# A larger part of a second stream's mixer is moved from ahead of a conditional to beside the experts behind it

## The chip, the core and the metric

One Trainium2 chip, one NeuronCore of it. The program is one launch: all weights and inputs lie in HBM, and the result goes back there. The metric is the device time of one execution in microseconds; a kernel's time is the median of its runs. The profiled execution is one more run, with the hardware profiler on; times inside the program are given in microseconds from its first instruction.

## The reference, cut to what matters

The program is two transformer blocks in a row, all in float32. The first block has two layers; each is an attention and a mixture of 16 experts (a token goes to 2 of them):

```python
for layer in range(DEPTH):
    sh1, sc1, g1, sh2, sc2, g2 = jnp.split(c_act @ w_mod[layer] + b_mod[layer], 6, axis=-1)
    ...
    x = x + g1[:, None, :] * mix
    h = modulate(rmsnorm(x, ffn_norm_g[layer]), sh2, sc2)
    x = x + g2[:, None, :] * grouped_moe(h, router_w, router_bias, exp_w_gate[layer], exp_w_up[layer], exp_w_down[layer])
```

The second block has two streams, `x` (256 tokens, from the first block) and a context `ctx` (256 tokens, an input). Its first layer works on the context by itself:

```python
hc = _rms(ctx, norm_mix_w[l]) * (1.0 + scc1) + shc1
qa_c, ka_c, va_c, qb_c, kb_c, vb_c = heads(hc @ w_in, False)
oa_c = _dense_attend(qa_c, ka_c, va_c, sink)
ob_c = _dense_attend(qb_c, kb_c, vb_c, None)
out_c = jnp.concatenate([oa_c, ob_c], axis=-1) @ w_out
ctx = ctx + gc1 * ac
ctx = ctx + gc2 * _swiglu(_rms(ctx, norm_ffn_w[l]) * (1.0 + scc2) + shc2, ffn_w_in[l], ffn_w_out[l])
```

None of this needs `x`. So the context's mixer (norm, projections, attention, output) and its feed-forward part can run at any time ahead of the second block's attention over both streams.

## The kernel before

The kernel writes its work as Python generators. A generator issues the instructions of a piece and yields a number, the piece's weight. `mix` (L236) takes several generators with a total weight each and always advances the one that is least far along; `upto` (L264) takes from one generator until a weight is used up; `then` runs one after the other; `drain` runs to the end. A scheduler then sets the order on each engine from the order in which instructions were written, their dependences and the buffers that are free. The order is fixed at build time: an engine takes its instructions in that order and waits where an operand is not there.

All weights come through SP's DMA queue, in units of 128 x 1024 float32 (512 KB), into a pool `raw` of eight buffers; a unit can be issued when the work that read the buffer before it is done. `wsplit` (L346) splits a unit into two parts H and L, one instruction on ACT (L356) and one on DVE (L357), and a matrix product `lin` (L371) is three matmuls for each 128 rows (L379 to L381): the high parts, and the two mixed ones. `lin_t` (L399 to L401) is the same with the operands exchanged, used for the values. Modulation vectors are made by `mods` (L553): a group has 16 units, each read by four matmuls straight from `raw` (L562), then one copy (L567) and four transpositions (L570).

The place of the change is the first block's first mixture of experts, in `run` (L1490 to L1501):

- `moe_route` norms `x`, routes each token and loads four units of the first expert pair into buffers of their own, `eraw`.
- `before` gathers the tokens of the first four experts (L907), writes the routing's remainder, drains what it is given as `fill`, loads eight more units of the first pair into `raw`, and calls `overflow` (L991).
- `overflow` is a conditional on all engines: its body runs when an expert got more than 64 tokens. Nothing is moved across it: what is written ahead of it stands ahead of it on every engine. In these inputs its body is jumped over. Its first instructions are the loads of the count `novi` (L1005) and the branch (L1006).
- `experts` runs eight pairs of experts: four bursts of sixteen records for gate and up (L388, out of `eraw` or `raw` into `psE`), an activation, transpositions (L947), two bursts for down, and the scatter back into `x` (L964, L965).

The context's mixer is the generator `con` = `context()`, which runs `even_mixer` (L1232) for `ctx` and then the norm for its feed-forward part. Its pieces, in order, are: the norm and the two projections of the keys (weight 5.3); the values (two units `wevv`, L399 to L401) and the keys' head norms (L1218, L1228; 7.0); the first query, two projections with `wev` units (2.6 each) and their head sums (1.3); then four rounds of attention (scores L1285 into the bank `psS`, transpositions L642, products L620) with the next query beside each, and the output projection with `wevo` units. `cffn.run(1)` is the first part of the context's feed-forward. `chain` holds two groups of modulation vectors, 32 units, whose results are needed later.

In this stage PSUM has three banks `psE`, one `psS` that the modulation groups use too, one `psZ`, and `psN` and `psL` from outside.

Of the kernel before, what the change touches and what calls it, by code (L numbers as in the profile page):

```python
# [235 lines left out]
def mix(*streams):  # L236

    live = [[g, 0.0, float(n)] for g, n in streams if g is not None]
    while live:
        s = min(live, key=lambda v: v[1] / v[2])  # L240
        try:
            n = next(s[0])
            s[1] += n
            yield n
        except StopIteration:
            live.remove(s)


def drain(g):
    for _ in g:  # L250
        pass


def then(*gs):
    for g in gs:
        yield from g
# [7 lines left out]
def upto(n, g):  # L264

    while n > 0:
        v = next(g, None)
        if v is None:
            return
        n -= v  # L270
        yield v
# [16 lines left out]
class Net:  # L288
# [1134 lines left out]
    def run(self, stop=None):  # L1423
# [32 lines left out]
        def hidden(u):  # L1456
            yield from self.swiglu(0, fx[0], fx[1], ctx, mc[0][:, 40:48], u, u + 1)

        cffn = Chain(*((u, hidden(u)) for u in range(11)))
        with ExitStack() as es1:  # L1460
# [11 lines left out]
            with ExitStack() as es:  # L1472
                self.banks(es, M=1, S=2, T=1, V=1)
                self.pools(es, ("big", 1), ("st", 1), ("wk", 1))
                chain = Chain(("gate", mod0([1])), ("c0", mod20([0])), ("m0", mod0([2])), ("c1", mod20([1])),
                              ("kv", self.mods(a["modkv"], [0], self.crep, self.v["bkv"], mk)))
# [7 lines left out]
            def context():  # L1484
                s = dict(x=ctx, m=mc[0], gate=iter(()), fill=iter(()))
                yield from self.even_mixer(self.fp, self.st, s, (kc, vvc), None)
                fx.extend(self.t(self.fp, [P, KD, S], tag, F32R) for tag in ("hh", "hl"))
                self.norm(ctx, KD, self.v["nfw0"], mc[0][:, 32:40], mc[0][:, 24:32], *fx)
# [3 lines left out]
            with ExitStack() as es:  # L1492
                self.banks(es, E=3, Z=1, S=1, M="S", D="S", T="Z", V="L", Y="L")
                self.extra = 4
                self.pools(es, ("eraw", self.extra), ("mo", 1), ("wk", 1), ("st", 1))
                chain = Chain(("c2", mod20([2])), ("m1", mod1([0])))
                con = context()
                drain(self.moe_route(0, self.v["ffng0"], m0))
                before, experts = self.moe_experts(mix((upto(18.0, con), 18), (chain.run(), 47)))
                drain(before)  # L1500
                drain(mix((experts, 196), (then(con, cffn.run(1)), 76)))  # L1501
            if stop == "moe0":
                return
            with ExitStack() as es:
# [3 lines left out]
                chain = Chain(("m1", mod1([1, 2])))  # L1508
# [3 lines left out]
            with ExitStack() as es:  # L1512
# [4 lines left out]
                before, experts = self.moe_experts(cffn.run(5))  # L1517
# [27 lines left out]
        with ExitStack() as es1:  # L1545
# [15 lines left out]
            with ExitStack() as es:  # L1561
# [3 lines left out]
                chain = Chain(("g", mod21([1])), ("f", mod21([2])))  # L1565
# [32 lines left out]
```

## Time and profile before

| | us |
|---|---|
| median of 3 runs | 2150.39 |
| lowest and highest run | 2146.48, 2150.41 |
| the profiled execution | 2157.56 |
| its span, first to last instruction | 2155.8 |
| first expert burst behind the conditional | 326.66 |
| the last expert pair's scatter begins | 677.18 |

In the timeline a row is an engine's stretch of like instructions: start, length, engine, line, operation, what it writes and reads, the count, and in brackets the idle time ahead of it with what ended it. A matmul's length there includes its way through the array; the price of one among many is the distance of their starts. A float32 matmul makes two records. PE is TensorE, PEld its weight loads, DVE VectorE, ACT ScalarE, POOL GpSimd; SPq is a row of SP's queue, an issued transfer.

### The profile page before, as it was taken

What the parts mean: (1) busy time and instruction counts of PE and PEld (TensorE: products, weight loads), DVE (VectorE), ACT (ScalarE), POOL (GpSimd) and SP (SyncE); (2) the same over time, 40 slices, a digit from 0 to 9 for tenths busy, and PEclk for the clock granted to TensorE, in tenths of its full rate; (3) what the DMA queues carried; (4) which work ended last, traced back from release to release, by engine and by line L of the source; (5) the groups of instructions that cost most, each with busy time, mean ns of one, the idle gap of its engine ahead of it and who ended that gap; (6) DMA issues with size and microseconds to landing.
All of it is one profiled execution on the core that took longest, in us unless ns stands there. A gap on an engine that the chain in (4) does not pass through costs nothing.

```text
span 2155.8 us, 35965 instructions
## 1 busy us (share of the span) xinstructions
PE 2006.3 (93%) x13942; PEld 1486.7 (69%) x13942; DVE 1201.8 (56%) x3193; ACT 835.2 (39%) x1580; POOL 134.2 (6%) x152
## 2 busy tenths in 40 slices
PE   5999889999998999999999989997999999998999
PEld 2666664544446877874555358777999777768999
DVE  3644643434345676752433257767777556576776
ACT  2343323433223355531222134755444334444443
POOL 1000200000002110100000014002000100001000
PEclk8999889999999999999999999998999999998999
DMA  9788678768787666438988976103555533224552
GB/s 369 264 301 313 256 255 323 282 248 346 283 349 286 215 224 218 163 130 333 366 345 353 410 277 242 69 20 137 181 185 173 171 139 118 98 94 145 187 183 93
DMA packets 135845, 492.84 MB, mean 229 GB/s; under 512 B 15136, under 2 KB 15536, under 8 KB 135408
## 3 DMA queue, kind: packets, MB, share of 16 engines
q1 hardware_dynamic: 134640, 487.63, 61.7%
q8 instruction: 113, 1.85, 0.3%
q10 hardware_dynamic: 864, 2.53, 0.3%
q0 software_dynamic: 160, 0.27, 0.1%
q14 instruction: 68, 0.56, 0.1%
HBM read 489.32 MB, written 1.05 MB: 227 GB/s over the span
## 4 chain that ended last, share of the span: by engine, by line
PE 48%; DVE 4%; DMA 2%; ACT 1%; issue 1%; POOL 0%; POOLq 0%; ACTq 0%; DVEq 0%
PE psL L379 8%; PE psL L380 8%; PE psL L381 8%; PE psE L388 7%; PE psM L562 1%; PE psS L1390 1%; PE psT L642 1%; PE psS L1285 1%; PE psD L379 1%; PE psD L381 1%; PE psD L380 1%; PE psV L620 1%; DVE L L357 1%; PE psL L399 1%; PE psL L401 1%
## 5 line engine op out<-in xcount | busy, mean ns | idle before, releaser
L379 PE MATMUL psL<-hh,H 128*128 128x256 f32 (+1 forms) x1800 | 535.4, 299 | 12.3 <-ACT H L356 3.4
L357 DVE TENSOR_TENSOR L<-raw,H 128x1024 fp32r<-128x1024 f32 (+1 forms) x336 | 409.7, 1222 | 231.3 <-ACT H L356 221.9
L381 PE MATMUL psL<-hh,L 128*128 128x256 f32 (+1 forms) x1800 | 525.4, 293 | 6.7 <-DVE L L357 6.7
L380 PE MATMUL psL<-hl,H 128*128 128x256 f32 (+1 forms) x1800 | 525.5, 293 | 4.4 <-DVE hl L489 4.0
L356 ACT CAST H<-raw 128x1024 fp32r<-128x1024 f32 (+1 forms) x336 | 347.5, 1039 | 424.3 <-PE psL L380 118.2
L379 PEld LDWEIGHTS psL<-hh,H 128*128 128x128 f32 x1800 | 352.1, 196 | 52.3 <-issue 23.2
L381 PEld LDWEIGHTS psL<-hh,L 128*128 128x128 f32 x1800 | 351.4, 196 | 19.6 <-DVE L L357 10.8
L380 PEld LDWEIGHTS psL<-hl,H 128*128 128x128 f32 x1800 | 351.6, 196 | 14.4 <-issue 5.4
L442 POOL TENSOR_TENSOR sa<-sa,sq 128x256 f32<-128x256 f32 x83 | 72.8, 877 | 1188.4 <-ACT sq L440 776.0
L562 PE MATMUL psM<-raw,crep 128*32 128x256 f32 x1408 | 125.7, 407 | 17.1 <-DVE crep L612 13.3
L388 PE MATMUL psE<-eraw,xg 128*64 128x512 f32 x512 | 125.5, 637 | 3.9 <-PEq L1006 3.8
L388 PE MATMUL psE<-raw,xg 128*64 128x512 f32 x512 | 116.0, 597 | 2.0 <-DMA raw<-in_eu_dram 2.0
L595 ACT ACTIVATE pr<-psS,nm,hr 128x512 f32<-128x512 f32 (+1 forms) x96 | 67.8, 706 | 72.5 <-DVE nm L589 45.2
L379 PE MATMUL psL<-ah,H 128*128 128x256 f32 x296 | 87.0, 297 | 5.8 <-DVE x L1174 2.1
L388 PE MATMUL psE<-raw,at 128*64 128x512 f32 x384 | 89.0, 601 | 2.1 <-ACT at L948 2.1
L388 PEld LDWEIGHTS psE<-eraw,xg 128*64 128x64 f32 x512 | 37.1, 145 | 72.7 <-issue 67.9
L380 PE MATMUL psL<-al,H 128*128 128x256 f32 x296 | 84.4, 286 | 0.7 <-DVE al L369 0.6
L381 PE MATMUL psL<-ah,L 128*128 128x256 f32 x296 | 83.1, 282 | 0.3 <-DVE L L357 0.3
L388 PEld LDWEIGHTS psE<-raw,xg 128*64 128x64 f32 x512 | 34.8, 137 | 65.6 <-issue 59.7
L562 PEld LDWEIGHTS psM<-raw,crep 128*32 128x32 f32 x1408 | 38.7, 113 | 56.5 <-issue 16.4
L586 DVE TENSOR_REDUCE mx<-psS 128x1 f32<-128x512 f32 (+1 forms) x80 | 46.1, 580 | 38.5 <-PE psS L1285 30.0
L379 PEld LDWEIGHTS psL<-ah,H 128*128 128x128 f32 x296 | 56.2, 191 | 13.9 <-DVE ctx L1174 4.7
(404 smaller groups left out, 3470.3 us busy)
## 6 DMA issues: line engine op xcount, KB each, us to landing
raw<-in_mod_dram SPq DMA_DIRECT2D x192, 512.0 KB, 4.8
raw<-in_ed_dram SPq DMA_DIRECT2D x96, 512.0 KB, 9.6
raw<-in_fg_dram SPq DMA_DIRECT2D x66, 512.0 KB, 4.3
raw<-in_fu_dram SPq DMA_DIRECT2D x66, 512.0 KB, 4.1
raw<-in_fo_dram SPq DMA_DIRECT2D x66, 512.0 KB, 3.9
eraw<-in_eg_dram SPq DMA_DIRECT2D x64, 512.0 KB, 7.7
raw<-in_eg_dram SPq DMA_DIRECT2D x64, 512.0 KB, 8.7
raw<-in_eu_dram SPq DMA_DIRECT2D x64, 512.0 KB, 7.4
```

Of the source, the lines that this page charges most:

```text
L356: nc.scalar.copy(h[:, :n], r[:, :n])
L357: nc.vector.tensor_tensor(l[:, :n], r[:, :n], h[:, :n].bitcast(F32), op=ALU.subtract)
L379: mm(ps[:, ns], wh, xh[:, k, ns], start=k == 0, stop=False)
L380: mm(ps[:, ns], wh, xl[:, k, ns], start=False, stop=False)
L381: mm(ps[:, ns], wl, xh[:, k, ns], start=False, stop=k == kt - 1)
L388: self.nc.tensor.matmul(o, w, r, start=start, stop=stop)
L399: mm(ps[:, :n], xh[:, kk, ts], w[0][:, k], start=kk == 0, stop=False)
L401: mm(ps[:, :n], xl[:, kk, ts], w[0][:, k], start=False, stop=kk == last)
L442: (nc.vector if i else nc.gpsimd).tensor_tensor(acc[i], acc[i], sq, op=ALU.add)
L562: nc.tensor.matmul(ps[32 * j:32 * j + 32, 256 * hf:256 * hf + 256], crep[:, k, :], r[:, 256 * j:256 * j + 256], start=k == 0, stop=k == KD ...
L586: V.reduce_max(mx, ps[:, :n], axis=AX.X)
L595: nc.scalar.activation(p, ps[:, :n], AF.Exp, bias=nm, scale=scale, accum_out=sm)
```

## The change

```diff
                 con = context()
                 drain(self.moe_route(0, self.v["ffng0"], m0))
-                before, experts = self.moe_experts(mix((upto(18.0, con), 18), (chain.run(), 47)))
+                before, experts = self.moe_experts(mix((upto(5.0, con), 5), (chain.run(), 47)))
                 drain(before)
-                drain(mix((experts, 196), (then(con, cffn.run(1)), 76)))
+                drain(mix((experts, 196), (then(con, cffn.run(1)), 89)))
```

Before, the pieces of `con` up to the first query's head sums are written ahead of the conditional (5.3 + 7.0 + 2.6 + 2.6 + 1.3 = 18.8). After, only the first piece is (5.3), and the others are written beside the experts. No instruction is added or taken away.

What it does to the order. On PE, ahead of the conditional, the last rows of before are two modulation units, a head sum of the first query, the last unit, its transposition and a score matmul of the context's attention:

```order
L381 MATMUL psL_3294<-hh_2815,L_3291 128x256
L562 MATMUL psS_3180<-raw_3328,crep_108 32x256 x4
L562 MATMUL psS_3180<-raw_3334,crep_108 32x256 x4
L1218 MATMUL psN_3372<-cst_64,sil_3320 128x2 x2
L562 MATMUL psS_3180<-raw_3340,crep_108 32x256 x4
L570 MATMUL psZ_3348<-cst_64,msb_3346 128x128 x4
L1285 MATMUL psS_5994<-kc,ah_3223 128x256
L1005 TENSOR_LOAD novi_2733
L1006 COMPARE_AND_BRANCH
```

Of these rows the query's projection (L381), its head sum (L1218) and the score matmul (L1285) moved behind the conditional.

Now the keys' head norms (sums L1218, spreads L1228) stand among the modulation units, and the last of these come in one row:

```order
L1228 MATMUL psN_5860<-cst_64,hr_5847 64x128 x4
L562 MATMUL psS_3070<-raw_3107,crep_108 32x256 x4
L1218 MATMUL psN_5866<-cst_64,sil_2962 128x2 x2
L562 MATMUL psS_3070<-raw_3113,crep_108 32x256 x4
L1228 MATMUL psN_5883<-cst_64,hr_5870 64x128 x4
L562 MATMUL psS_3070<-raw_3119,crep_108 32x256 x4
L562 MATMUL psS_3070<-raw_3125,crep_108 32x256 x4
L562 MATMUL psS_3070<-raw_3131,crep_108 32x256 x4
L562 MATMUL psS_3070<-raw_3137,crep_108 32x256 x4
L570 MATMUL psZ_3169<-cst_64,msb_3167 128x128 x4
L1005 TENSOR_LOAD novi_2733
L1006 COMPARE_AND_BRANCH
```

Four more such units stand between the last L562 shown and L570. What moved is the work that stood between the units: only the keys' norms are left.

On PE, just behind the conditional, the first burst reads `eraw` in both kernels. Before, a score matmul, a transposition of the context's attention and then the burst of the four `raw` units that were loaded first follow:

```order
L388 MATMUL psE_5985<-eraw_2568,xg_2738 64x512
L388 MATMUL psE_5985<-eraw_2566,xg_2738 64x512
L1285 MATMUL psS_5995<-kc,ah_3223 128x256
L642 MATMUL psZ_6058<-cst_64,pr_6003 128x128
L388 MATMUL psE_5985<-raw_3396,xg_2738 64x512
L388 MATMUL psE_5985<-raw_3394,xg_2738 64x512
```

The context's attention rows between the bursts moved to the second pair and later.

Now the burst of the units loaded last (3183 to 3189) follows at once, then that of the units loaded first (3175 to 3181), then the values:

```order
L388 MATMUL psE_5770<-eraw_2566,xg_2738 64x512
L388 MATMUL psE_5897<-raw_3189,xg_2738 64x512
L388 MATMUL psE_5897<-raw_3187,xg_2738 64x512
L388 MATMUL psE_5897<-raw_3185,xg_2738 64x512
L388 MATMUL psE_5897<-raw_3183,xg_2738 64x512
L388 MATMUL psE_5770<-raw_3181,xg_2738 64x512
L388 MATMUL psE_5770<-raw_3179,xg_2738 64x512
L388 MATMUL psE_5770<-raw_3177,xg_2738 64x512
L388 MATMUL psE_5770<-raw_3175,xg_2738 64x512
L399 MATMUL psL_5791<-H_5781,hh_2815 128x256
L400 MATMUL psL_5791<-L_5782,hh_2815 128x256
L401 MATMUL psL_5791<-H_5781,hl_2816 128x256
```

The values moved here from ahead of the conditional, and the two `raw` bursts changed places.

In SP's queue the value units stood ahead of the last six units of the first modulation group. Now the modulation units and the eight expert units stand there without a break up to SP's load of the count, and behind the conditional come, in this order:

```order
L343 DMA eraw_5906<-in_eu_dram 128x1024
L343 DMA eraw_5908<-in_eu_dram 128x1024
L343 DMA eraw_5910<-in_eu_dram 128x1024
L335 DMA raw_5779<-in_wevv_dram 128x1024
L335 DMA raw_5785<-in_wevv_dram 128x1024
L343 DMA eraw_5912<-in_eu_dram 128x1024
L335 DMA raw_5940<-in_ed_dram 128x1024
```

The value units moved from ahead of the conditional to behind three transfers of the first pair. From the last expert pair's first scatter matmul (677.18 us before) to the end of the program PE's rows are the same in both kernels, and in the same order.

## Rows read from the trace of the kernel before

**Rows 1.** The page: TensorE's row; the two instructions of a weight unit's split.

```profile
PE 2006.3 (93%) x13942; PEld 1486.7 (69%) x13942; DVE 1201.8 (56%) x3193; ACT 835.2 (39%) x1580; POOL 134.2 (6%) x152
L357 DVE TENSOR_TENSOR L<-raw,H 128x1024 fp32r<-128x1024 f32 (+1 forms) x336 | 409.7, 1222 | 231.3 <-ACT H L356 221.9
L356 ACT CAST H<-raw 128x1024 fp32r<-128x1024 f32 (+1 forms) x336 | 347.5, 1039 | 424.3 <-PE psL L380 118.2
```

**Rows 2.** Windows: length; busy PE, PEld, DVE, ACT, POOL; clock; DMA share; GB/s.

```profile
264.00:282.30 18.30, 15.21 (x119) 9.65 (x111) 9.38 (x40) 3.58 (x8) 0.00 (x0) 0.87 0.74 253
282.30:290.93 8.63, 8.63 (x66) 7.33 (x66) 5.66 (x15) 4.70 (x11) 0.00 (x0) 0.88 0.59 194
290.93:304.21 13.28, 12.48 (x134) 9.51 (x131) 4.83 (x21) 2.38 (x5) 0.00 (x0) 1.00 0.69 234
304.21:320.70 16.49, 13.75 (x112) 10.42 (x109) 5.04 (x24) 1.79 (x3) 0.00 (x0) 0.83 0.91 353
320.70:326.66 5.96, 4.54 (x35) 2.22 (x35) 2.49 (x14) 2.03 (x3) 0.00 (x0) 0.79 0.51 190
326.66:677.18 350.52, 328.71 (x1698) 168.68 (x1699) 141.33 (x422) 119.01 (x253) 5.12 (x7) 0.98 0.79 308
```

**Rows 3.** PE's timeline around the conditional: start, length, instruction, count, idle ahead.

```profile
289.91 1.07 PE L562 MATMUL psS<-raw,crep 128*32 128x256 f32 x16
290.93 0.39 PE L399 MATMUL psL<-H,hh 128*128 128x256 f32 x1
...
296.79 0.51 PE L1218 MATMUL psN<-cst,sil 128*128 128x2 f32 x4
...
298.66 0.66 PE L570 MATMUL psZ<-cst,msb 128*128 128x128 f32 x4 [0.80 <-DVE msb L567]
...
300.66 0.66 PE L1228 MATMUL psN<-cst,hr 128*64 128x128 f32 x8
...
324.70 0.66 PE L570 MATMUL psZ<-cst,msb 128*128 128x128 f32 x4 [1.27 <-DVE msb L567]
325.29 1.22 PE L1285 MATMUL psS<-kc,ah 64*128 64x256 f32 x2
326.66 6.34 PE L388 MATMUL psE<-eraw,xg 128*64 128x512 f32 x16
...
337.41 0.70 PE L1285 MATMUL psS<-kc,ah 64*128 64x256 f32 x2
```

**Rows 4.** PE's timeline, a 24-matmul projection and a burst in the experts' stretch.

```profile
605.75 0.39 PE L379 MATMUL psL<-hh,H 128*128 128x256 f32 x1
...
608.82 3.65 PE L388 MATMUL psE<-raw,xg 128*64 128x512 f32 x16
```

**Rows 5.** Transfers: landing time of units issued 282 to 290 us; a full window.

```profile
raw<-in_mod_dram SPq DMA_DIRECT2D x3, 512.0 KB, 3.2
305.00:310.00 5.00, 4.47 (x40) 3.54 (x44) 1.29 (x7) 0.22 (x1) 0.00 (x0) 1.00 1.02 399
```

**Rows 6.** PE's waits, 326.66 to 677.18 us: us in total, times, longest.

```profile
PE psS L1285 <- ACT pr L595: 4.0, 3, 1.7
...
PE psZ L964 <- DVE x L966: 1.9, 7, 0.3
PE psN L964 <- DVE x L966: 1.9, 4, 0.5
PE psN L964 <- ACT mh L959: 1.8, 3, 0.8
```

**Rows 7.** PE's timeline, the last expert pair's first scatter matmul.

```profile
677.18 0.28 PE L964 MATMUL psN<-SG,mh 128*128 128x256 f32 x1
```

## The prediction

> **What bounds the kernel now.** I read the page first, then the windows by stage, then TensorE's timeline on either side of the conditional. The page has PE busy 93% of the span [rows 1], so what decides is where PE's remaining idle time and its slow clock lie, not how much work there is. The stretch that the change touches runs from about 264 us (the router is done, the first gather starts) to 677.18 us, where the last expert pair is scattered back [rows 7]. The windows cut it in two at the conditional [rows 2]. Ahead of it, 264.00 to 326.66, PE is busy 54.6 of 62.7 us (the five rows added). Behind it, 326.66 to 677.18, PE is busy 328.7 of 350.5 us, with the granted clock at 0.98 of full speed and the DMA engines at 0.79: the experts are bound by PE, and a microsecond of PE work that is put there costs about a microsecond. The reader should see two more things. Ahead of the conditional the granted clock falls to 0.83 and 0.79 in the last two rows, and the DMA rate swings between 194 and 353 GB/s: neither PE nor DMA runs full there. And the first burst behind the conditional takes 6.34 us [rows 3], where a burst of the same sixteen records takes 3.65 us later [rows 4]: PE is at 1.2 GHz there and not at 2.4.
>
> From the last pair on, the order of PE's instructions is the same in both kernels. So the whole change is the shift of that one point, 677.18 us: how much earlier the conditional comes, less what the experts' stretch grows by.
>
> **How much earlier the conditional comes.** Before, the context's work between its first two projections and the conditional is: the values (48 matmuls, 290.93 to 296.79 us, 5.9 us), the first query's two projections (48 matmuls) and two small head sums (L1218). Also one score matmul, L1285, at 325.29 us, is ahead of the first burst at 326.66 us [rows 3]. All of it leaves. What stays ahead of the conditional is the norm, the two projections of the keys with their head norms, and all 32 units of the two modulation groups. The change says what it does: the order shows the values and the query behind the conditional, and the head norms of the keys still ahead of it.
>
> I rebuild the new stretch from rows. The context's two key projections end at 289.9 us, where the next modulation rows start [rows 3]; two modulation units now stand ahead of them, and a unit is eight records, so by 1.07 us for sixteen records [rows 3] that is 1.07 us: they end at about 291.0. Behind them stand sixteen modulation units (128 records, 8.6 us), two head sums and two head spreads (0.5 and 0.6 us each, L1218 and L1228), two transpositions of a modulation row (0.6 each, L570) and the two waits for the copy ahead of those (0.80 and 1.27) [rows 3]. That is 8.6 + 3.4 + 2.1 = 14.1, so PE alone would be done at 305.1 us.
>
> The transfers say a little later. There are eight `raw` buffers and two hold the context's norm until about 288 us, so about eight of these sixteen units can be on the way when PE gets to them, and the other eight wait for a buffer. The ninth is issued when the first has been read, about 292.7 us; one alone takes 3.2 us to land [rows 5], so 296 us; the next seven follow at the rate that the DMA engines reach when they are kept full, 399 GB/s [rows 5], which is 1.31 us for 512 KB: 305.2 us. Reading the last (0.5), the copy (1.27) and the transposition (0.6) make 307.6. I take 307.5 us for the first expert burst, **19.2 us earlier**. The bounds are 305.1 (PE alone) and, with the 253 GB/s of the first window [rows 2], 2.07 us for a unit, 310.5 + 2.4 = 312.9: between 21.6 and 13.8 us earlier.
>
> The Trainium skill, DMA: Bandwidth & Descriptors, section "Where 436 GB/s comes from", says that transfers from HBM are held to about 358 GB/s for a core. By that the eight units take 1.46 us each and the conditional would come 1.2 us later. The row has 399 GB/s over 5 us, so the trace does not agree for a stretch of that length.
>
> **What the experts' stretch pays.** PE work at full clock: values 5.9; the query's two projections, by one of 24 matmuls from 605.75 to 608.82 us [rows 4], 6.1; the two head sums 1.1; the score matmul that stood at 325.29 us, 0.7, as the one at 337.41 us takes [rows 3]. Together **13.8 us**. ACT and DVE get four more splits of a weight unit (1.04 and 1.22 us each [rows 1]) and SP four more transfers; ACT is busy 119 and DVE 141 of 350 us there, and the DMA engines are at 0.79 [rows 2], so these are hidden but for the first pair.
>
> At the first pair they are not. The eight units of experts that stand last ahead of SP's branch follow the modulation units through the same buffers: at 1.31 us each the last lands at 305.2 + 8 x 1.31 = 315.7 us. The first burst, from buffers of its own, ends at 307.5 + 6.3 = 313.8 us, and the second now is the one that reads the units loaded last: 1.9 us of waiting. The third ends at 323.0. Then come the 48 matmuls of the values, whose two weight units SP issues behind three transfers into `eraw` and as `raw` buffers come free in the second burst, near 317.5 us; landed 3.2 later and split on ACT and DVE (1.04 + 1.22 [rows 1]), the first is ready at 323.0, and about half a unit later behind the transfers that are queued: 0.6 us. **2.5 us** together. The lower bound is 0; if the first value unit waits for a buffer of the third burst, it is 5.
>
> The rest of the stretch moves both ways. PE's waits there in the row view are 1.9 + 1.9 + 1.8 us ahead of the scatter's first matmuls L964 and 4.0 us ahead of the score matmuls L1285 [rows 6]. Counted in PE's order over the eight pairs, an L964 follows another scatter matmul at once 29 times before and 15 times now, since there is more projection work to put between: 5.6 x 14/29 = 2.7 us less. But two score matmuls that share the one `psS` bank stand within about 2 us of each other five times before and nine times now: 4.0 x 4/5 = 3.2 us more. I set the two at 0.5 us more, with -2.7 and +3.2 as ends.
>
> **The sum.** -19.2 + 13.8 + 2.5 + 0.5 = -2.4 us on the profiled execution, whose span is 2155.8 us and whose time is 2157.56. The median of the runs is 2150.39, 7.2 us less, and the stretch is no different there for all that is known; I put the same shift on it: **2148.0 us**, 0.1% faster. A measurement of this kernel tells about 0.2%, 4.3 us, from no change, so the forecast is "no change".
>
> The Trainium skill, TensorE: Matmul & The Clock Gate, section "Loop structure matters more than you think", says that matmuls which wait for DMA let PE go cold, and that the matmul after it runs cold. That speaks against this change, which makes PE wait for modulation units between 296 and 306 us. Before, the granted clock is 0.79 in the window ahead of the first burst and that burst is slow already [rows 2, 3], so the sum has one slow burst either way; by the rule a second burst at 1.2 GHz would add 6.34 - 3.65 = 2.7 us and make the sum +0.3 us, still no change.
>
> **Rivals.** *The gaps fill (faster).* The conditional comes when PE alone allows it (305.1 us, -21.6), the added projections cover the scatter's waits (-2.7), the score matmuls cost nothing more and the first pair waits 2.5: -21.6 + 13.8 + 2.5 - 2.7 = -8.0 us, 2142.4. For it: the experts' stretch has 21.8 us of idle PE, which is all in small waits, and more independent work stands between them now. Against it: the eight modulation units that must still come through two-thirds of the buffers after 291 us, and the one score bank.
>
> *The transfers set the pace (slower).* From the ninth modulation unit to the value weights, 21 units come through one queue in a row. If they come not at 399 but at the experts' mean of 308 GB/s [rows 2], 1.70 us for a unit, the last modulation unit lands at 307.9 us (+2.7), the last of the eight expert units at 321.5, the second burst starts there, and the five units behind it land at 330, so the values start near 332.3 and not 323.6: +8.7 us, a sum of +6.3 us, 2156.7. It turns slower than 0.2% at about 1.61 us for a unit, 326 GB/s. For it: the mean rates of the rows ahead of the conditional, 253, 194 and 234 GB/s. Against it: in those rows PE held the buffers, and where several transfers were queued the rate was 399.
>
> **How the numbers follow.** Forecast 0.48, filled gaps 0.36, transfers 0.16. The forecast's own range is -7 to +2 us, by the bounds of its terms; a little of it lies past 0.2% on the faster side, and a little of the filled gaps (those under 4.3 us) on this side. So faster 0.40, the same 0.45, slower 0.15. The range reaches from -10 to +5 us, 2140.4 to 2155.4: it leaves out the far end of the filled gaps and most of the slower rival, and takes in the bounds of the unknown terms.
>
> **What would show it.** In the profile of the changed kernel the first burst of L388 behind the conditional should start at 305 to 309 us; the modulation rows ahead of it should show waits on `raw<-in_mod_dram` of a few us in all; a wait on `raw<-in_eu_dram` of 1 to 3 us should stand ahead of the second burst; the values (L399) should run at 323 to 330 us; and the last pair's scatter should start near 675 us. It would be wrong if the first burst started after 311 us (the transfers), if that scatter came before 671 us (the gaps fill), or if the span changed outside this stretch, where the order is the same.

## The result, and the profile after

The changed kernel takes 2169.51 us in the median (2168.22 to 2172.92) where the kernel before takes 2150.1: a ratio of 1.0095, 95% interval 1.0081 to 1.0110. It is 19.4 us, 0.95%, slower; the forecast was 2148.0 and "no change". The profiled execution took 2172.92 us with a span of 2171.1, 15.3 more than the span before; the profiled execution of before is 7 us above its median, that of after 3.4.

First the page: TensorE's row, to be held against [rows 1]. The share is the same, the busy time is 11.5 us more for the same number of instructions.

```profile
PE 2017.8 (93%) x13942; PEld 1490.2 (69%) x13942; DVE 1199.0 (55%) x3193; ACT 834.0 (38%) x1580; POOL 134.9 (6%) x152
```

Then the windows by stage, as in [rows 2] (length; busy PE, PEld, DVE, ACT, POOL; clock; DMA share; GB/s). The cuts are where the context's key projections begin and end, where the last modulation units are waited for, and the first burst behind the conditional.

```profile
264.00:284.30 20.30, 18.04 (x150) 10.85 (x142) 9.99 (x48) 2.88 (x8) 0.00 (x0) 0.84 0.77 253
284.30:295.40 11.10, 11.07 (x56) 8.40 (x56) 5.04 (x14) 3.91 (x10) 0.00 (x0) 0.75 0.46 154
295.40:308.60 13.20, 10.67 (x133) 5.88 (x132) 5.27 (x29) 0.48 (x2) 0.00 (x0) 0.87 0.88 330
308.60:314.40 5.80, 2.57 (x28) 0.90 (x29) 0.87 (x2) 0.00 (x0) 0.00 (x0) 1.00 1.02 412
...
314.42:696.80 382.38, 354.54 (x1804) 186.28 (x1805) 145.78 (x450) 125.25 (x264) 5.78 (x7) 0.94 0.76 290
```

The last row is the experts' stretch, from the first burst to the last pair's first scatter matmul, which stood at 677.18 us before [rows 7]. It is 382.38 us long against 350.52. TensorE is busy 25.8 us more in it and idle 6.0 us more, and the granted clock is 0.94 where it was 0.98 [rows 2].

TensorE's timeline around the conditional, for [rows 3], and at the end of the stretch:

```profile
308.62 0.64 PE L562 MATMUL psS<-raw,crep 128*32 128x256 f32 x8 [0.43 <-DMA raw<-in_mod_dram]
310.31 0.64 PE L562 MATMUL psS<-raw,crep 128*32 128x256 f32 x8 [1.05 <-DMA raw<-in_mod_dram]
311.60 0.64 PE L562 MATMUL psS<-raw,crep 128*32 128x256 f32 x8 [0.65 <-DMA raw<-in_mod_dram]
313.05 0.66 PE L570 MATMUL psZ<-cst,msb 128*128 128x128 f32 x4 [0.81 <-DVE msb L567]
314.42 2.76 PE L388 MATMUL psE<-eraw,xg 128*64 128x512 f32 x11 [0.72 <-PEq L1006]
320.11 2.46 PE L388 MATMUL psE<-eraw,xg 128*64 128x512 f32 x5 [2.92 <-issue]
322.38 7.83 PE L388 MATMUL psE<-raw,xg 128*64 128x512 f32 x32
333.72 0.38 PE L399 MATMUL psL<-H,hh 128*128 128x256 f32 x1 [3.51 <-ACT H L356]
334.98 0.58 PE L400 MATMUL psL<-L,hh 128*128 128x256 f32 x1 [0.87 <-DVE L L357]
...
696.80 0.28 PE L964 MATMUL psN<-SG,mh 128*128 128x256 f32 x1
```

The first burst starts 12.2 us earlier than before. Inside it TensorE stands for 2.92 us with nothing that the profile shows to wait for. The values then wait 3.51 and 0.87 us for the split of their weights. Why the weights are late is on SP's queue:

```profile
306.01 3.09 SPq L335 DMA_DIRECT2D raw<-in_eg_dram  x4
309.19 3.43 SPq L335 DMA_DIRECT2D raw<-in_eu_dram  x4
322.90 2.86 SPq L343 DMA_DIRECT2D eraw<-in_eu_dram  x3
325.87 0.84 SPq L335 DMA_DIRECT2D raw<-in_wevv_dram  x2
```

The value units stand behind three transfers into `eraw`, which go out when the first burst gives its buffers back (322.90 us), and are issued at 325.87, not near 317.5 as forecast. TensorE's waits from the first burst to 696.80 us, for [rows 6]:

```profile
PE psS L1285 <- ACT pr L595: 6.9, 6, 1.8
PE psL L399 <- ACT H L356: 3.5, 1, 3.5
PE psE L388 <- issue: 2.9, 1, 2.9
...
PE psN L964 <- ACT mh L959: 0.3, 1, 0.3
```

The scatter's waits of 5.6 us (L964) are all but gone, and the score matmuls wait 6.9 us for the softmax where they waited 4.0. So far the idle time. The clock is seen when the stretch is cut where it changes. These are windows in which it is low; the long rows between them, 341 to 385, 406 to 450, 454 to 501, 512 to 549 and 556 to 668 us, have 1.00. Two more low windows are not shown: 320 to 324 us, in the first bursts, and 668 to 672 (0.58), behind a wait of 1.29 us for expert weights.

```profile
334.00:341.00 7.00, 6.13 (x29) 6.02 (x29) 2.06 (x2) 2.87 (x4) 0.00 (x0) 0.51 1.03 416
...
385.00:389.00 4.00, 4.00 (x14) 1.73 (x16) 1.93 (x12) 1.70 (x4) 0.00 (x0) 0.57 0.98 393
399.00:406.00 7.00, 5.69 (x15) 2.71 (x17) 1.85 (x8) 2.60 (x8) 0.00 (x0) 0.51 1.00 392
...
450.00:454.00 4.00, 4.00 (x12) 1.08 (x10) 1.39 (x7) 2.50 (x6) 0.00 (x0) 0.57 1.02 419
501.00:512.00 11.00, 10.40 (x24) 3.15 (x26) 3.71 (x12) 3.18 (x11) 0.00 (x0) 0.53 0.79 306
...
549.00:556.00 7.00, 6.52 (x17) 2.47 (x18) 1.43 (x3) 2.43 (x5) 0.00 (x0) 0.51 1.02 411
```

Each of the windows shown follows a wait: the values' at 333.72 us, a wait of 0.68 for the scatter matrix at 384.61, and the score matmuls' of 1.77 (399.63), 0.76 and 1.12 (446.44, 448.92), 1.53 (501.24) and 0.91 us (547.63). One of them in TensorE's timeline:

```profile
497.75 0.70 PE L1285 MATMUL psS<-kc,ah 64*128 64x256 f32 x2
498.37 0.33 PE L947 MATMUL psE<-cst,ga 128*128 128x128 f32 x1
498.63 1.08 PE L620 MATMUL psL<-pt,vvc 128*64 128x256 f32 x6
501.24 1.09 PE L1285 MATMUL psS<-kc,ah 64*128 64x256 f32 x2 [1.53 <-ACT pr L595]
...
508.26 3.61 PE L388 MATMUL psE<-raw,at 128*64 128x512 f32 x8
511.69 3.60 PE L388 MATMUL psE<-eraw,xg 128*64 128x512 f32 x16
```

The second score matmul of a pair follows the first by less than 3 us of other work, finds the one `psS` bank still under the softmax and waits 1.53 us. For the 10 us behind it TensorE runs at 1.2 GHz: eight records of L388 take 3.61 us there, sixteen take 3.60 from 511.69 on.

Not every wait is followed by a low clock. The sixth score wait of the changed kernel, 0.76 us at 594.02, is not: the clock is 1.00 from 556 to 668 us. And of the three in the kernel before only one is:

```profile
436.94 0.70 PE L1285 MATMUL psS<-kc,al 64*128 64x256 f32 x2 [1.70 <-ACT pr L595]
437.57 5.35 PE L388 MATMUL psE<-eraw,xg 128*64 128x512 f32 x16
...
452.34 0.70 PE L1285 MATMUL psS<-kc,ah 64*128 64x256 f32 x2 [1.09 <-ACT pr L595]
452.97 3.65 PE L388 MATMUL psE<-raw,at 128*64 128x512 f32 x16
```

The burst behind the wait of 1.70 us takes 5.35 us, those behind the waits of 1.09 and of 1.20 us (541.59) take 3.65, full speed. What decides this is not shown by any run here.

The account of the +19.6 us at the end of the stretch: the first burst -12.2; moved work at full clock +13.8, as forecast; idle time +6.0; and 25.8 - 13.8 = 12.0 us by which the same matmuls took longer, which is the clock. From that point to the end the rows are the same in both kernels, and yet the changed one takes 4.3 us less there (1474.3 against 1478.6); so the two profiled executions differ by 15.3 us in the end, and that 19.6 comes so near to the 19.4 of the medians is in part chance.

### The profile page after: what moved, and what is told of

Its sections match the earlier page's. It is cut to its first block, busy times and chain, and to the rows that moved or that the text cites. A ratio compares the mean times of both kernels' runs of the same rounds, so it can differ in the third digit from the quotient of the medians.

```text
span 2171.1 us, 35956 instructions
## 1 busy us (share of the span) xinstructions
PE 2017.8 (93%) x13942; PEld 1490.2 (69%) x13942; DVE 1199.0 (55%) x3193; ACT 834.0 (38%) x1580; POOL 134.9 (6%) x152
## 4 chain that ended last, share of the span: by engine, by line
PE 47%; DVE 4%; DMA 1%; ACT 1%; issue 1%; POOL 0%; POOLq 0%; ACTq 0%; DVEq 0%
PE psL L379 8%; PE psL L380 8%; PE psL L381 8%; PE psE L388 7%; PE psM L562 1%; PE psS L1390 1%; PE psT L642 1%; PE psS L1285 1%; PE psD L379 1%; PE psD L381 1%; PE psD L380 1%; PE psV L620 1%; DVE L L357 1%; DMA raw<-in_fg_dram 1%; PE psL L399 1%
## 5 line engine op out<-in xcount | busy, mean ns | idle before, releaser
L381 PE MATMUL psL<-hh,L 128*128 128x256 f32 (+1 forms) x1800 | 524.4, 293 | 5.0 <-DVE L L357 5.0
L381 PEld LDWEIGHTS psL<-hh,L 128*128 128x128 f32 x1800 | 350.2, 195 | 18.1 <-DVE L L357 8.7
L562 PE MATMUL psM<-raw,crep 128*32 128x256 f32 x1408 | 126.5, 411 | 16.3 <-DVE crep L612 13.2
L388 PE MATMUL psE<-eraw,xg 128*64 128x512 f32 x512 | 122.3, 619 | 7.2 <-PEq L1006 4.1
L388 PE MATMUL psE<-raw,xg 128*64 128x512 f32 x512 | 118.4, 607 | 2.4 <-DMA raw<-in_eu_dram 2.4
L388 PE MATMUL psE<-raw,at 128*64 128x512 f32 x384 | 96.6, 640 | 2.2 <-ACT at L948 2.1
L388 PEld LDWEIGHTS psE<-eraw,xg 128*64 128x64 f32 x512 | 36.3, 142 | 73.2 <-issue 68.2
L381 PE MATMUL psL<-ah,L 128*128 128x256 f32 x296 | 83.4, 283 | 0.3 <-DVE L L357 0.3
L388 PEld LDWEIGHTS psE<-raw,xg 128*64 128x64 f32 x512 | 35.9, 139 | 68.7 <-issue 62.0
L562 PEld LDWEIGHTS psM<-raw,crep 128*32 128x32 f32 x1408 | 39.1, 114 | 56.2 <-issue 17.8
L399 PE MATMUL psL<-H,hh 128*128 128x256 f32 x224 | 64.7, 292 | 3.5 <-ACT H L356 3.5
```

Of the source, the lines that this page charges most:

```text
L381: mm(ps[:, ns], wl, xh[:, k, ns], start=False, stop=k == kt - 1)
L388: self.nc.tensor.matmul(o, w, r, start=start, stop=stop)
L399: mm(ps[:, :n], xh[:, kk, ts], w[0][:, k], start=kk == 0, stop=False)
L562: nc.tensor.matmul(ps[32 * j:32 * j + 32, 256 * hf:256 * hf + 256], crep[:, k, :], r[:, 256 * j:256 * j + 256], start=k == 0, stop=k == KD ...
```

## The experiments

Each kernel was timed beside the kernel before. The table has the median, the ratio to before with its interval, and from the profile the start of the first burst behind the conditional, the length from there to the first burst of the second expert layer, TensorE's busy time in it, and the score matmuls' waits for the softmax (rows L1285 or L1283 with ACT pr). The bank edit and the hold are explained below. A profile is one execution; those of "cut 5, weight 100" and "cut 5, bank, values loaded" are of their kernels' shortest execution.

| kernel | us | ratio | first burst | length | busy | score waits |
|---|---|---|---|---|---|---|
| before (cut 18, weight 76) | 2150.1 | | 326.66 | 637.4 | 599.0 | 4.0 |
| changed (cut 5, weight 89) | 2169.5 | 1.0095 [1.0081, 1.0110] | 314.42 | 668.3 | 625.2 | 6.9 |
| changed, once more | 2169.3 | 1.0096 [1.0079, 1.0112] | 313.14 | 665.7 | 624.8 | 6.9 |
| cut 18, weight 89 | 2150.6 | 1.0006 [0.9995, 1.0016] | 324.58 | 636.3 | 600.8 | 1.8 |
| cut 12 | 2149.4 | 0.9999 [0.9987, 1.0011] | 314.20 | 646.6 | 608.6 | 1.8 |
| cut 5, weight 76 | 2177.7 | 1.0124 [1.0105, 1.0143] | 314.08 | 676.2 | 622.1 | 5.0 |
| cut 5, weight 100 | 2164.8 | 1.0075 [1.0058, 1.0092] | 312.16 | 654.4 | 614.2 | 0.6 |
| cut 5, values loaded | 2170.5 | 1.0101 [1.0083, 1.0119] | 314.64 | 665.8 | 624.8 | 6.9 |
| cut 18, bank | 2142.4 | 0.9970 [0.9958, 0.9981] | 325.52 | 626.6 | 593.1 | 1.5 |
| cut 5, bank | 2149.1 | 0.9998 [0.9987, 1.0008] | 314.11 | 646.1 | 612.2 | 0.0 |
| cut 12, bank | 2149.4 | 1.0007 [0.9994, 1.0019] | 313.66 | 640.2 | 602.7 | 0.0 |
| cut 5, bank, values loaded | 2148.9 | 0.9997 [0.9986, 1.0009] | 310.41 | 645.1 | 612.2 | 0.0 |
| cut 5, bank, hold | 2156.4 | 1.0037 [1.0023, 1.0052] | 313.73 | 652.2 | 611.3 | 4.0 |
| **cut 12, bank, hold** | **2134.3** | **0.9936 [0.9920, 0.9953]** | 315.51 | 627.8 | 595.2 | 0.0 |
| cut 18, bank, hold | 2153.2 | 1.0008 [0.9993, 1.0024] | 324.88 | 640.2 | 600.7 | 0.2 |
| cut 12, hold | 2154.0 | 1.0019 [1.0009, 1.0028] | 314.08 | 650.3 | 612.5 | 2.9 |
| cut 5, hold | 2161.2 | 1.0059 [1.0037, 1.0082] | 311.89 | 653.9 | 614.7 | 5.5 |

**Half of the change, and the weight alone.** Two theories stood at the start: F, that the loss is made at the first pair by the values, and C, that it is made all along the stretch by the attention's waits and the clock.

```
cut 12:              upto(12.0, con), 12   ...   then(con, cffn.run(1)), 82
cut 18, weight 89:   upto(18.0, con), 18   ...   then(con, cffn.run(1)), 89
```

> Half of the change: the cut stands at 12 and the weight of the context's stream is 82, so the two value units and their 48 matmuls stay ahead of the conditional and only the first query, its head sums and the first score matmul go beside the experts. Theory F (the loss of the full change is made at the first pair: 2.92 us of idle TensorE in the first burst, 3.51 and 0.87 us ahead of the values, and values at 1.2 GHz): all of that is tied to the values, so this kernel is 2 to 7 us faster than the kernel before. Theory C (the loss is made all along the experts' stretch, where TensorE falls to 1.2 GHz after waits of the context's attention): the attention still begins later and is still packed closer than before, so 3 to 9 us slower than before, and the granted clock of the experts' stretch is near 0.95 rather than 0.98.

> The kernel before with the weight 89 for the context's stream instead of 76 and nothing moved across the conditional: the stream is paced 17% faster against the experts. Theory C: what counts is how close the attention's waits stand to each other, so 3 to 8 us slower than before, with more of the experts' stretch at 1.2 GHz. Theory F: no change within 3 us, the first pair being the same.

The half step is neither: the time of the kernel before to 0.1%. Its timeline of TensorE says why, and tells something on the branch too:

```profile
310.01 0.64 PE L562 MATMUL psS<-raw,crep 128*32 128x256 f32 x8 [0.63 <-DMA raw<-in_mod_dram]
311.28 0.64 PE L562 MATMUL psS<-raw,crep 128*32 128x256 f32 x8 [0.63 <-DMA raw<-in_mod_dram]
312.74 1.11 PE L570 MATMUL psZ<-cst,msb 128*128 128x128 f32 x4 [0.81 <-DVE msb L567]
314.20 6.20 PE L388 MATMUL psE<-eraw,xg 128*64 128x512 f32 x16 [0.35 <-PEq L1006]
320.22 7.05 PE L388 MATMUL psE<-raw,xg 128*64 128x512 f32 x32
333.29 0.58 PE L379 MATMUL psL<-hh,H 128*128 128x256 f32 x1 [6.03 <-ACT H L356]
```

The stall is 6.03 us and now stands ahead of the query: it belongs to whichever context unit comes first behind the conditional, not to the values. And with the values still ahead of the conditional, the first burst stands at 314.20 us, where the full change has it. The start of a profile shifts by up to 2.8 us from one execution to the next (the matmul of L446, ahead of the change, stands between 276.16 and 278.94 us in the seventeen profiles). Counted from L446, the first burst comes after 36.7 to 37.8 us in the four profiles with the cut at 12 and after 34.3 to 35.9 in the nine with the cut at 5: 5.9 us of values moved across brought the conditional forward by about 1 to 2 us. The last modulation units come one in 1.27 us, 512 KB each, 413 GB/s, and TensorE waits for them at either cut. With the cut at 18 the weight alone changes nothing, against theory C's 3 to 8 us.

**The bank.** The score matmuls of a head's two tiles of tokens went through the single `psS` bank one at a time. The edit puts both tiles of one half of the head into the two halves of the bank, so that a handover serves two.

```diff
-                for t in range(2):
+                for j in range(0 if is_x else 2):
+                    r = slice(64 * j, 64 * j + 64)
+                    ps = self.psum("S")
+                    for t in range(2):
+                        nc.tensor.matmul(ps[:, S * t:S * t + S], qt[r, mm, t * P:(t + 1) * P], own[0][r, ab],
+                                         start=True, stop=True)
+                    for t in range(2):
...
+                        p, rc = self.softmax(ps[:, S * t:S * t + S], nk, rq[mm][:, t, j:j + 1], sink=sink)
...
+                for t in range(2 if is_x else 0):
```

It is made for the context's attention alone (`is_x` is false there).

> The changed kernel with one edit: in the context's attention the two score matmuls of one head half (two tiles of tokens) write the two halves of one PSUM bank and are followed by their two softmaxes, where before each took the single bank for itself and waited for the softmax of the one ahead; half as many handovers of the bank. Theory C: 5 to 13 us faster than the changed kernel, the waits of L1285 on the softmax below 4 us (6.9 in the changed kernel) and less of the stretch at 1.2 GHz. Theory F: no more than the waits themselves, 0 to 3 us faster than the changed kernel.

> The same edit of the context's score matmuls in the kernel before. Theory C: 0 to 5 us faster than before, clearly less than what the same edit gives the changed kernel, since the kernel before has about 12 us of the stretch at 1.2 GHz and the changed one 44. Theory F: 0 to 3 us faster than before, the same as in the changed kernel.

In the changed kernel the edit is worth 20.4 us (2169.5 to 2149.1), in the kernel before 6.8 (2149.2 to 2142.4). The windows of the changed kernel, from the first burst behind the conditional to that of the second expert layer, without and with the edit:

```profile
314.42:982.70 668.28, 625.22 (x3870) 418.56 (x3871) 350.75 (x994) 261.56 (x539) 42.44 (x46) 0.96 0.67 249
```

```profile
314.11:960.20 646.09, 612.21 (x3870) 417.86 (x3870) 347.43 (x994) 261.07 (x539) 41.74 (x46) 0.97 0.69 258
```

Both have 3870 records on TensorE. It is busy 13.0 us less with the edit and idle 9.2 less; the score waits are 0.0 of 6.9, and the low windows near 399, 450, 501 and 549 us are gone. Those at 320, 334 and 385 us stay, one at 480 (0.57 for 4 us) is new, and the first pair's stalls (2.7, 4.0 and 0.7 us) are still there. Theory C fits, with a larger gain than the 5 to 13 us that it was given. It is no proof that the waits alone did it, since the edit also changes the order of the whole stretch. With the bank edit in both, the cut at 5 still costs 6.7 us more than the cut at 18; that this is the first pair's share was not shown apart.

**Once more.** Was the low clock that one execution's?

> The changed kernel once more, without an edit, for a second profile. Theory C (the loss is TensorE at 1.2 GHz behind waits that the order of the instructions makes): 2166 to 2173 us again, and the low stretches lie at the same places within a few us (near 334, 385, 399, 450, 501 and 549 us), 40 to 55 us of them in the experts' stretch, against 12 in the kernel before. Rival N (the low clock of the first profile was that execution's own): the low stretches lie elsewhere, or sum to less than 25 us.

Four of the second profile's low windows:

```profile
332.00:340.00 8.00, 6.97 (x33) 6.78 (x34) 2.36 (x2) 3.29 (x5) 0.00 (x0) 0.57 1.02 415
...
397.00:405.00 8.00, 6.17 (x17) 2.86 (x19) 2.23 (x11) 2.67 (x8) 0.00 (x0) 0.57 1.01 404
...
500.00:511.00 11.00, 10.64 (x26) 3.03 (x27) 3.24 (x12) 3.31 (x8) 0.00 (x0) 0.54 0.81 320
547.00:555.00 8.00, 7.33 (x23) 3.04 (x22) 1.92 (x4) 2.59 (x5) 0.00 (x0) 0.57 1.01 400
```

Each stands 1 to 2 us ahead of its place in the first profile, as the first burst does, and so do those near 384 and 449 us. Behind the conditional the low windows sum to some 43 us at half clock, 44 in the first profile (windows of 1 us). For these six windows the low clock goes with the order of the instructions, and rival N is out. It is not so for all: the window at 668 us of the first profile is missing in the second, and the first burst is at half clock there from 312 to 319 us, where the first profile has the full clock up to 320.

**Other interleaves of the same work.** Weight 76 and weight 100 with the cut at 5.

> The changed kernel's cut at 5 with the weight of the kernel before, 76 instead of 89: the same work is moved behind the conditional, the interleave with the experts is another. Theory C1 (the price is that of the moved work as such: the attention's waits and the clock suffer whenever the attention starts later): within 4 us of the changed kernel, some 2166 to 2173 us. Theory C2 (the price comes of how this one interleave places the score matmuls against their softmaxes, and another interleave has other waits): 5 to 15 us away from the changed kernel, with the waits of L1285 and the time at 1.2 GHz moving together with the time.

> The changed kernel with the weight 100 instead of 89, a third interleave of the same work. Theory C1: within 4 us of the changed kernel, or slower by up to 8 where density counts. Theory C2: again another number of waits of L1285 and another time, which follows the microseconds at 1.2 GHz in the experts' stretch (44 in the changed kernel) at about half a microsecond for each.

They are 8.2 us above and 4.7 below the changed kernel, 27 and 14 above the kernel before. Which score matmul waits differs, as C2 has it, but all three are clearly slower than before, and the time does not follow the score waits. At weight 76 they are 5.0 us, less than in the changed kernel, and TensorE is busy 3.1 us less; the longest wait there is another, 8.63 us ahead of L454, a norm, at 693.47 us: the last scatter row stands at 681 us, and from 684 to 694 TensorE is busy 1.1 of 10 us. At weight 100 they are 0.6 us, but in a profile of 2159.41 us with a mean clock of 0.969, only 1.9 us longer than that of the kernel before; its other three executions took 2164 to 2166 us at 0.965 to 0.966 and have no profile.

**The first pair.** The two value units take the place of two expert units among the eight loads ahead of the branch.

```diff
-            early.extend(self.eload(src) for src in srcs[self.extra:8 + self.extra])
+            n = 8 + self.extra - len(units)
+            early.extend(self.eload(src) for src in srcs[self.extra:8])
+            self.loaded.update((str(u), self.wload(u, U)) for u in units)
+            early.extend(self.eload(src) for src in srcs[8:n])
```

> The changed kernel with the two value units loaded ahead of the conditional, in place of two of the eight expert units that stood there (which follow later): the values no longer wait for SP to get buffers from the first bursts. Theory F (the first pair's share of the loss is the late load of the value units): the wait of L399 for the split (3.51 and 0.87 us) goes and with it the stretch at 1.2 GHz behind it, 4 to 8 us faster than the changed kernel; the stall in the first burst stays. Rival F2 (the first pair is bound by the transfers, and two expert units that come later cost what the values gain): within 2 us of the changed kernel, with a new wait of L388 for the raw units.

> Both edits, the score matmuls of two token tiles in one bank and the value units loaded ahead, in the changed kernel. If the loss is the sum of the first pair's (F, about 7 us) and the attention's (C, about 13 us), this kernel comes to 2141 to 2146 us, level with the kernel before with the bank edit (2142.4) and 4 to 8 us below the changed kernel with the bank edit (2149.1). Rival F2: 2147 to 2151 us, no gain on top of the bank edit.

No gain, alone or with the bank edit. The values begin at 324.2 us and not at 333.7, but still wait 2.52 us for the split, and the query's first unit then waits 1.37: as rival F2 has it, what one unit gains another gives back.

**Holding the context's stream.** `later(8.0, ...)` lets two more bursts go ahead of the first context unit (its cost is added to the weight). With the cut at 12:

```diff
-                drain(mix((experts, 196), (then(con, cffn.run(1)), 82)))
+                drain(mix((experts, 196), (later(8.0, then(con, cffn.run(1))), 90)))
```

> The bank edit with the cut at 12 and weight 82: values ahead of the conditional, the first query behind it. Theory G (with the attention's waits gone, an earlier conditional pays what it saves, and the price of the change is the stall of the first context unit behind the conditional, whichever it is): the stall of some 6 us at the query's first unit stays, as in the half step without the bank edit, and the time is 2141 to 2145 us, level with the kernel before with the bank edit (2142.4). Theory F (the stall belongs to the values): no stall, 2136 to 2140 us.

> The changed kernel with the bank edit, and the context's stream held back for two more bursts of the experts (a cost of 8 ahead of it, weight 97), so that the value units are asked for behind five bursts and not behind three. Theory G (the first context unit stalls because its weights stand in SP's queue behind units that wait for the first bursts' buffers): the wait of L399 for the split is below 1 us and the time 3 to 7 us below that of the bank edit alone (2149.1), 2142 to 2146 us. Rival T (the first pair is bound by its transfers, whatever stands where): the wait goes to the bursts, L388 waits for raw units instead, 2147 to 2152 us.

> The bank edit, the cut at 12 and the context's stream held back for two more bursts (weight 90). Theory G: 3 to 7 us below the same kernel without the hold, 2135 to 2141 us, the fastest of all. Rival T: no gain from the hold, 2140 to 2146 us.

Without the hold, cut 12 gets nothing from the bank edit (2149.4, above both forecasts; its first unit still waits 4.56 us). With it, 2134.28 us: 0.64% faster than the kernel before, the fastest of all and below both forecasts. TensorE behind its conditional:

```profile
315.51 5.26 PE L388 MATMUL psE<-eraw,xg 128*64 128x512 f32 x16 [0.81 <-PEq L1006]
323.73 7.09 PE L388 MATMUL psE<-raw,xg 128*64 128x512 f32 x32 [2.95 <-SPq L1006]
332.25 3.65 PE L388 MATMUL psE<-eraw,xg 128*64 128x512 f32 x16 [1.43 <-DMA eraw<-in_eu_dram]
...
337.31 3.70 PE L388 MATMUL psE<-raw,at 128*64 128x512 f32 x16
340.94 0.33 PE L947 MATMUL psE<-cst,ga 128*128 128x128 f32 x1
341.03 0.36 PE L379 MATMUL psL<-hh,H 128*128 128x256 f32 x1
```

The query starts at 341.03 us without a wait, though two bursts ahead of it now wait 2.95 and 1.43 us, as rival T has it. From its first burst to the second expert layer this kernel needs 627.8 us where the kernel before needs 637.4, though it holds the query's work too: its clock there is 0.99. For cut 5 with the bank edit the same hold lost 7 us (2156.4, above both forecasts): L399's wait is gone, but a score matmul waits 2.97 us at 534.98, and a norm 3.33 at 647.08.

Which of the three edits did it?

> Cut at 12 and hold of 8 (weight 90), without the bank edit. If the hold alone repairs the half step (the stall of the query's first unit and the 10 us at 1.2 GHz behind it), 8 to 15 us below the half step without the hold (2149.4), 2134 to 2141 us, with or without score waits. If it takes both edits, because the score matmuls' waits on the softmax are again among the bursts, 2144 to 2152 us.

> The kernel before with the bank edit and the same hold of 8 (weight 84), the cut left at 18. If the hold is a better interleave whatever stands ahead of the conditional, some 5 to 8 us below the bank edit alone (2142.4), 2134 to 2138 us, level with the kernel that has all three edits (2134.3). If the gain of the three edits is that of the earlier conditional, once its first stall and the score waits are gone, no gain here: 2140 to 2146 us, since no weight unit stands first behind this conditional.

> The changed kernel (cut at 5, two score matmuls one after the other through one bank) with the hold of 8 and weight 97. With the bank edit the hold cost this cut 7 us. If the price of the full change lies in how the attention stands against the bursts, another interleave moves the score waits and the low clock but does not remove them: 2155 to 2175 us. If it lies in the first pair, whose stall the hold removes: 2160 to 2164 us with the score waits unchanged at some 7 us.

No two of them give as much. At cut 18 the bank edit alone is worth 6.8 us; the cut at 12 alone is worth nothing, and neither is the cut with the bank edit. The hold alone at cut 18 was not run. The hold costs 4.7 us at cut 12 without the bank edit and 10.8 at cut 18 with it, and gains 15.1 at cut 12 with it. The cut at 12 with the hold and the cut at 18 with both edits are slower than either forecast for them. The edits do not add: every one makes the scheduler order the whole stretch anew. The changed kernel with the hold lies within both its forecasts, 8.3 us below the changed kernel with 5.5 us of score waits left.

## Why the prediction was wrong

By its own signs the forecast failed: the first burst stands behind 311 us, the values at 333.7 us and not at 323 to 330, the last pair's scatter at 696.80 us and not near 675, and the same instructions behind that point took 4.3 us less.

**The conditional comes earlier: -19.2 forecast, -12.2 measured.** 2.0 us of the difference is in the trace ahead of the change (the wait ahead of L446 stands at 278.79 us, at 276.76 before). From there on the first burst is 14.3 us earlier, near the forecast's far bound of 13.8; the three other profiles with the cut at 18 need 47.6 us from L446 to the first burst where that of the kernel before needs 49.9, and against these it is 12.0. Two things failed. The key projections were set down to end at 291.0 us and end at 295.4, of which 2.0 are the later start: the row from 284.3 has the clock at 0.75 against 0.88 in the second of [rows 2], and no term priced that. And the transfers run at 154 GB/s in that row, presumably because TensorE gives buffers back at that pace; afterwards, at 330 and 412, the units are waited for. The 399 GB/s was right for a full queue, but the queue filled later. That is the rival "the transfers set the pace" in its first half, and the half step shows it best: most of the 5.9 us of values hides behind those transfers where it stands ahead of the conditional.

**The moved work: +13.8.** It was not measured apart, and the 12.0 us of the clock rest on it. Windows of 1 us give another estimate: behind the conditional they have some 44 us at half clock after and 12 before, which would be 16 us had TensorE been busy all through; then the moved work cost about 10 and the clock more. The bank edit gives a size without it: 13.0 us of busy time for the same 3870 records.

**The first pair: +2.5 forecast, 7.3.** 2.92 us in the first burst and 3.51 and 0.87 ahead of the values are 7.3. The forecast had the value units issued when the second burst frees `raw` buffers; SP is in order, and three transfers into `eraw` ahead of them waited for the end of the first burst, which the 2.92 us had made late. The wait on `raw<-in_eu_dram` ahead of the second burst did not come.

**Scatter and score waits: +0.5 forecast, -2.4 measured.** -5.3 (5.6 to 0.3) and +2.9 (4.0 to 6.9), for -2.7 and +3.2. Counting neighbours in the order was sound, for the waits.

**The clock: not in the sum, +12.0.** This is the step that turned the sign. The forecast priced the clock at one burst (+2.7, and left it out of the sum), charged all work behind the conditional at 2.4 GHz because the row said 0.98, and took the score waits at their own length. They were 6.9 us long, 2.9 more than before, and the growth of the low clock is four times that. Of the 44 us at half clock some 27 stand behind five of these six waits, the rest in the first pair, at 385 and at 668 us; before, one window of 4 us stands behind a score wait. The timed executions agree in kind: the mean granted clock is 0.971 before and 0.962 after (medians of the runs beside the second profile), and time times clock has the medians 2086.9 us before and 2087.5 after. This reckoning is rough, as it halves idle time in a low window too; by the account above the clock is 12.0 of the 19.6 us. The Trainium skill, TensorE: Matmul & The Clock Gate, section "A second HAM failure mode: psum-queue depth-cycling", tells of a kernel that goes round PSUM banks and idles for short times between groups of matmuls, so that the clock swings; the trace agrees for five of the six waits of 0.8 to 1.8 us at one bank (the low windows above), and not for the sixth. The prediction had weighed only that page's rule on waits for DMA.

With +7.0, +4.8, -2.9 and +12.0 the forecast's -2.4 becomes 18.5, against the 19.6 of the profile; the 1.1 left are small waits that no term had (idle time grew by 6.0, and 7.3 - 2.4 of it are named).

**What stays open.** The bank edit shows that the waits and the low clock go together; it also reorders the stretch, so no run here holds the order and changes the clock alone. Edits that only change the order moved the time by up to 15.1 us either way (the weights and the hold), and the bank edit gave 20.4, 6.8 and nothing at the three cuts; how much of its 20.4 us is the waits and how much a luckier order is open. Keeping TensorE busy through the waits was not tried, since added matmuls change the order too. Why some waits of about a microsecond are followed by the low clock and others are not, and why the hold helps two kernels and hurts three, is not settled.

## What to carry to other kernels

A wait on TensorE can cost more than its length, by the clock behind it, and a mean clock of 0.98 says nothing on what new waits will do: look for the windows at half clock, what stood ahead of each, and whether the change puts more such places into the stretch. A single buffer that is handed back and forth (here one PSUM bank between a score matmul and its softmax) is worth mending before work is moved next to it: it paid at two of three cuts. What is moved out of a stretch that transfers set the pace of brings little, here 1 to 2 us for 5.9. The first unit that needs its weights behind a branch stalls whichever it is; letting other work go first removed that stall, but made two of four such kernels faster and two slower. Where every edit makes a new order, a gain is to be measured for the whole and not added up.

## What the runs showed of the hardware

In all nine profiles with the cut at 5, the first burst behind the branch stops after its 11th record and goes on 5.5 to 6.1 us after its start, at full clock (2.92 us idle) or at half (0.42): the second profile has the eleven records in 5.35 us and the other five from 318.90. At the other cuts the sixteen run through. In the changed kernel three packets of one instruction queue and one of the other lie between 316.5 and 320.5 us beside data at 326 GB/s, so it looks like instructions that arrive late; that is argued, not shown. The half step has as many packets of these queues between 314.0 and 320.5 us as the changed kernel between 314.4 and 320.5, and its burst does not stop.

Transfers reached 412 to 419 GB/s in windows of 4 to 7 us (rows above).
